# Strassen's algorithm in the input product of two middle FFNs, S5 coefficients made early, modulations on TensorE

## The chip, the cores and the metric

One Trainium2 chip, one of its cores. The metric is device time of one execution in microseconds (us). The engines of the core work side by side, each in its own order: PE (TensorE, the matrix products), DVE (VectorE), ACT (ScalarE), POOL (GpSimd), SP (SyncE, which issues most DMAs). PEld is the loading of weights into PE, a row of its own in the profile. Measured beside each other, two runs of this kernel can be told apart from about 0.2% on.

## The reference

Two layers over 512 latent and 256 context tokens, width 1024. Each layer: a SwiGLU FFN at half weight, a mixer of four head groups (S5, neighbourhood attention, GQA, RG-LRU), and a second SwiGLU FFN. Shift, scale and gate of each come from a product of the condition with `w_ada` (1024 x 9216 for each layer), the "modulations".

```python
def ada_mods(s, w, b, dt):                 # s: silu(c), one row for latents, one for context
    m = (s @ w + b)                        # 1024 -> 9 * 1024
def ffn_half(h, g, w_i, w_o, shift, scale, gate):
    y = modulate(rms_norm(h, g), shift, scale)
    a, b = jnp.split(y @ w_i, 2, axis=-1)  # w_i: 1024 x 2 * 2816
    return h + FFN_RES * gate * ((jax.nn.silu(a) * b) @ w_o)
for l in range(DEPTH):                     # latents and context alike, with their own modulations
    h = ffn_half(h, g_ffn1[l], w_ffn1_in[l], w_ffn1_out[l], m[0], m[1], m[2])
    h = h + m[5] * (mixers(modulate(rms_norm(h, g_mix[l]), m[3], m[4]) @ w_in[l]) @ w_out[l])
    h = ffn_half(h, g_ffn2[l], w_ffn2_in[l], w_ffn2_out[l], m[6], m[7], m[8])
return rms_norm(h_lat, g_final)            # the second layer's last steps: latents alone
```

The S5 group needs, for each layer, tables and weights that depend on its parameters alone (`s5_discretize` and powers of its result): the "S5 coefficients".

## The kernel before

**Products.** The residual lies transposed, eight tiles of 128 channels x 768 tokens. A float32 product is made from two parts of each operand: three products, `hi * xl`, `lo * xh`, `hi * xh` (`mm`, L389). For each weight tile of 128 x 128 and each of the three, the 768 tokens go through PE in two instructions, since one takes 512 columns at most: 258 (two of them the shifts, so that the bias comes along) and 512. The parts of the weights are made where they are needed (`wsplit`): ACT copies a tile to `wh` (L378), DVE subtracts (`wl`, L379), 1024 elements wide for eight weight tiles. `wh` and `wl` have two buffers each, so a set can be made as soon as the set before the last has been used up.

**FFN.** `ffn` goes through 22 column tiles `f` of the hidden width. For each, `ff_in` makes the gate's and the value's product (eight weight tiles each: 2 x 48 matmuls, `pi`), DVE multiplies by the norm's factor `R` (L449, L453) and combines (L455), ACT applies silu (L451) and copies the high part (L458), POOL makes the low part (L459). After each group of column tiles (`FF`: five groups of 5, 5, 4, 4 and 4) the output product of the group follows for each of eight column tiles `j` (`po`), and DVE adds it to the residual (L495). With the last group the residual of tile `j` is final: `hg_tile` makes the parts of the next stage's operand at once (ACT L304, DVE L305, squares ACT L316, their sum POOL L317), while PE goes on with `j + 1`.

**Beside it.** Closures in `hooks` are traced between column tiles. `ada_steps`: 512 columns of the modulations each (a "group" below; 32 of them: 14 in the first FFN, 9 in the second FFN of layer 0, 9 in the first of layer 1). DVE multiplies and adds 16 times (two rows, eight row blocks; L254, L256), PE sums over the partitions (L263) and transposes (L268). The first four groups' worth are made during the start on PE instead (`ada_first`, L215: two rows of weights `s2`, 512 columns moving, into four strips of 32 PSUM partitions). `S5Coef.steps`: 23 closures for each layer, in the first FFN of its own layer, `S5_AT = 7`, `S5_BY = 13`: from column tile 7 on, over 13 tiles; POOL makes the weights (L1544 to L1546), PE transposes them.

**Order.** The program is written in this order, and a scheduler with its own timeline then orders each engine's instructions; buffers are given out from pools (`wraw`: raw weights, three buffers of 8 KB a partition; `wb`: the parts). Each engine then runs its list in order: an instruction that waits holds up those behind it on its engine.

## Time and profile before

| | |
|---|---|
| device time, three runs | 2876.4, 2879.5, 2881.92 us; median 2879.5 |
| span of the profiled execution, first to last instruction | 2877.7 us |
| PE busy | 2819.1 us, 98% |
| PE's loading of weights | 2437.7 us, 85% |
| DVE busy | 1742.3 us, 61% |
| ACT busy | 906.5 us, 32% |
| POOL busy | 757.7 us, 26% |
| DMA | 312.13 MB, 31.8% of 16 engines on SP's queue |

The stages, in us from the first instruction: start to 64; first FFN of layer 0 to 655; its mixer to 945 and output projection to 1020; second FFN of layer 0 to 1607; first FFN of layer 1 to 2186; mixer to 2490; second FFN of layer 1, latents alone, to the end at 2877.7.

A busy PE is not a PE at its peak: matmuls overlap in it and their ends are modelled, so that one record of 0.4 us can follow another after 0.24. What an instruction costs PE is read from start to start. Rows of a timeline merge neighbours of the same kind (the count behind the x); a figure in square brackets is idle time ahead of the row and what ended it.

### The profile page before, as it was taken

To read this page: it belongs to the slowest core of one execution; us is meant where nothing else is said; L and a number is where in the kernel's file an instruction comes from. 1 tells how busy PE (TensorE), PEld (TensorE's weight loads), DVE (VectorE), ACT (ScalarE), POOL (GpSimd) and SP (SyncE) were. 2 spreads that over 40 slices of the span, in tenths; PEclk is the share of its full clock that TensorE was granted. 3 is DMA by queue.
4 is the path that set the end of the run, shared out by engine and by line. 5 is a ranking of instruction groups with operands and counts; after the bars stand their busy time and mean duration, and the time that the engine had idled before them with its cause. 6 is when DMAs were issued, how large, how long until landed. Compare 5 with 4: busy or idle time off the path is not lost.

```text
span 2877.7 us, 43478 instructions
## 1 busy us (share of the span) xinstructions
PE 2819.1 (98%) x17293; PEld 2437.7 (85%) x17293; DVE 1742.3 (61%) x3178; ACT 906.5 (32%) x1478; POOL 757.7 (26%) x957
## 2 busy tenths in 40 slices
PE   7999999999999999999999999999999999999998
PEld 4888888888877888888888888888888887899998
DVE  6868577676857566363634766465466876444445
ACT  4212121235546422112123321222224645322223
POOL 2822233221323311000001176332312434201001
PEclk9999999999999999999999999999999999999999
DMA  6445324353323333222311335233254343232231
GB/s 227 134 108 167 112 96 141 123 185 118 115 62 74 103 115 99 87 96 95 107 54 54 118 101 142 80 123 106 74 168 145 118 106 89 79 96 83 88 96 52
DMA packets 295901, 312.13 MB, mean 108 GB/s; under 512 B 58991, under 2 KB 243202, under 8 KB 295698
## 3 DMA queue, kind: packets, MB, share of 16 engines
q1 hardware_dynamic: 266990, 293.97, 31.8%
q0 software_dynamic: 5664, 12.59, 1.9%
q10 hardware_dynamic: 23044, 2.78, 0.7%
q8 instruction: 137, 2.24, 0.3%
q14 instruction: 66, 0.54, 0.1%
HBM read 276.09 MB, written 29.02 MB: 106 GB/s over the span
## 4 chain that ended last, share of the span: by engine, by line
PE 88%; DVE 6%; DMA 2%; ACT 2%; issue 1%; POOL 0%; SPq 0%; ACTq 0%; DVEq 0%; POOLq 0%
PE pi L389 51%; PE po L389 23%; PE po L1236 4%; DVE acc L256 2%; PE po L862 2%; PE pt L810 2%; DMA wa<-in_w_ada_dram 1%; PE ps L793 1%; PE pa L263 1%; DVE wl L379 1%; PE ps L794 1%; DMA l<-in_w_ada_dram 1%; PE pl L734 1%; DVE z L455 0%; PE pa L215 0%
## 5 line engine op out<-in xcount | busy, mean ns | idle before, releaser
L389 PE MATMUL pi<-g,wh 128*128 128x258 f32 (+2 forms) x6656 | 1408.7, 330 | 8.4 <-ACT wh L378 2.6
L389 PEld LDWEIGHTS pi<-g,wh 128*128 128x128 f32 x6656 | 1101.4, 191 | 132.2 <-issue 15.0
L389 PE MATMUL pi<-g,wl 128*128 128x258 f32 (+2 forms) x3328 | 828.1, 329 | 0.7 <-DVE wl L379 0.7
L378 ACT CAST wh<-wr 128x1024 fp32r<-128x1024 f32 (+3 forms) x380 | 338.2, 890 | 1397.4 <-PE pi L389 674.8
L389 PEld LDWEIGHTS pi<-g,wl 128*128 128x128 f32 x3328 | 607.4, 191 | 60.6 <-issue 2.5
L389 PE MATMUL po<-l,wh 128*128 128x512 f32 (+1 forms) x2464 | 566.1, 344 | 0.9 <-DVE e L495 0.8
L389 PEld LDWEIGHTS po<-l,wh 128*128 128x128 f32 x2464 | 387.9, 188 | 63.9 <-issue 3.9
L459 POOL TENSOR_TENSOR l<-z,l 128x768 fp32r<-128x768 f32 (+1 forms) x88 | 159.1, 1808 | 1061.4 <-ACT l L458 955.4
L379 DVE TENSOR_TENSOR wl<-wr,wh 128x1024 fp32r<-128x1024 f32 (+3 forms) x380 | 407.0, 1071 | 50.3 <-ACT wh L378 47.5
L256 DVE SCALAR_TENSOR_TENSOR acc<-wa,s,acc 128x512 f32<-128x512 f32 x448 | 358.6, 849 | 39.4 <-DMA wa<-in_w_ada_dram 38.6
L495 DVE SCALAR_TENSOR_TENSOR e<-po,gt,e 128x512 f32<-128x512 f32 (+1 forms) x296 | 176.2, 631 | 307.4 <-PE po L389 250.7
L389 PE MATMUL po<-l,wl 128*128 128x512 f32 (+1 forms) x1232 | 337.5, 343 | 1.0 <-DVE wl L379 1.0
L453 DVE TENSOR_TENSOR z<-pi,R 128x768 f32<-128x768 f32 (+2 forms) x91 | 78.4, 865 | 301.3 <-PE pi L389 301.3
L389 PEld LDWEIGHTS po<-l,wl 128*128 128x128 f32 x1232 | 194.5, 188 | 32.6 <-DVE wl L379 2.0
L448 DVE COPY bc<-pi 128x2 f32<-128x2 f32 x88 | 13.7, 156 | 189.4 <-PE pi L389 189.4
L458 ACT CAST l<-z 128x768 fp32r<-128x768 f32 (+1 forms) x88 | 68.8, 782 | 160.5 <-DVE z L455 160.5
L1545 POOL TENSOR_TENSOR ww<-AR,BB 128x256 f32<-128x256 f32 x32 | 25.9, 808 | 341.4 <-PE pw L1564 309.5
L455 DVE SCALAR_TENSOR_TENSOR z<-z,pi,z 128x512 f32<-128x512 f32 (+1 forms) x154 | 107.1, 730 | 5.5 <-ACT z L451 0.7
L317 POOL TENSOR_TENSOR ssq<-ssq,sq 128x768 f32<-128x768 f32 (+1 forms) x35 | 67.5, 1929 | 161.0 <-ACT sq L316 161.0
L451 ACT ACTIVATE z<-z,bc 128x512 f32<-128x512 f32 (+1 forms) x154 | 90.0, 625 | 62.7 <-DVE z L449 51.3
L449 DVE TENSOR_TENSOR z<-pi,R 128x768 f32<-128x768 f32 (+1 forms) x88 | 77.5, 880 | 3.7 <-ACT R L366 3.7
L1236 PE MATMUL po<-l,wh 128*128 128x512 f32 (+1 forms) x264 | 71.9, 356 | 0.0
(349 smaller groups left out, 2632.0 us busy)
## 6 DMA issues: line engine op xcount, KB each, us to landing
wr<-in_w_ffn_in_dram SPq DMA_DIRECT2D x88, 1024.0 KB
wa<-in_w_ada_dram SPq DMA_DIRECT2D x64, 1024.0 KB
wr<-in_w_ffn_out_dram SPq DMA_DIRECT2D x48, 512.0 KB
wr<-in_w_ffn_out_dram SPq DMA_DIRECT2D x32, 640.0 KB
wr<-in_w_in_dram SPq DMA_DIRECT2D x16, 1024.0 KB
W<-s5w SPq DMA_DIRECT2D x32, 256.0 KB
wr<-in_w_out_dram SPq DMA_DIRECT2D x8, 1024.0 KB
l<-in_w_ada_dram SPq DMA_DIRECT2D x24, 256.0 KB
```

Source lines behind the costliest of these rows:

```text
L256: nc.vector.scalar_tensor_tensor(acc[r], raw[:, k], s, acc[r], ALU.mult, ALU.add)
L378: nc.scalar.copy(hi[:, :kn], raw[:, :, o:o + P])
L379: nc.vector.tensor_sub(lo[:, :kn], raw[:, :, o:o + P], hi[:, :kn].bitcast(F32))
L389: nc.tensor.matmul(dst, lhsT=wt[:, k, :], rhs=xt[:, a:b], start=(k == 0 and i == 0), stop=(k == kn - 1 and i == 2))
L449: nc.vector.tensor_mul(ta[:, :nt], pa[:, 256:256 + nt], self.R[:, :nt])
L451: nc.scalar.activation(ta[:, a:b], ta[:, a:b], AF.Silu, bias=bc[:, i:i + 1])
L453: nc.vector.tensor_mul(tb[:, a:b], p, self.R[:, a:b])
L455: nc.vector.scalar_tensor_tensor(tb[:, a:b], tb[:, a:b], pb[:, 254 + i:255 + i], ta[:, a:b], ALU.add, ALU.mult)
L458: nc.scalar.copy(uh[:, :nt], tb[:, :nt])
L459: nc.gpsimd.tensor_sub(ul[:, :nt], tb[:, :nt], uh[:, :nt].bitcast(F32))
L495: self.nc.vector.scalar_tensor_tensor(self.h[j][:, a:b], ps[:, a:b], gate[:, j, i:i + 1], self.h[j][:, a:b], ALU.mult, ALU.add)
L1236: self.nc.tensor.matmul(dst, lhsT=wt[:, k, :], rhs=xt[:, a:b], start=(c == 0 and i == 0), stop=(c == NT - 1 and i == 2))
```

## The change

1. **Strassen** (`STRASSEN`): in the second FFN of layer 0 and the first of layer 1 the input product of a column tile is taken as a 2 x 2 by 2 x 2 product of blocks: gate and value columns, even and odd row blocks (weights: `a11`, `a12`, `a21`, `a22`, 4 x 128 elements each), first and second half of the tokens. Seven products of four row blocks, three parts and one half of the tokens (386 or 384 columns) take the place of eight: 84 matmuls a tile, where 96 were.
   - `st_weights`: four sets of weight parts a tile instead of two: `ra` (1024 wide), `s12` (1024), `ra` again after two differences in place (1024), `a22` (512). POOL makes the four sums and differences, 512 wide each.
   - `st_in`: ACT copies the first product, DVE adds the other six with seven instructions, POOL multiplies by `R` (two of 768), ACT and DVE finish as before.
   - `st_tile` in place of `hg_tile`, once for each pair of residual tiles: ACT writes the four blocks, the sums and differences of blocks go to POOL (DVE for the last pair), seven splits follow (a copy on ACT and a difference on DVE, 386 wide each).
2. **Modulations on TensorE** (`ada_steps`): for each group eight float32 matmuls, 32 columns of weights (`s2w`, the two rows and what lies behind them), 512 columns moving, into strips `32 * (k % 4)` of one bank, in place of DVE's 16 instructions; ACT copies 512 columns; four matmuls against `sel` (128 x 2, sums over the strips) replace the two transposes.
3. **S5** (`S5_AT = (5, 14)`, `S5_BY = 7`): the coefficients of both layers are made in the first FFN of layer 0, each over seven column tiles.
4. **Room**: `FF` is (4, 4, 4, 4, 3, 3), the last group three instead of four; weights are loaded 128 columns wide (rows of 512 bytes), five raw buffers of 4 KB; `wh`, `wl` two buffers and `ws` one; the `z` tiles' pool is closed in the Strassen FFNs, where their place holds operand tiles (`x`); the tokens of ordinary products go in halves (386 + 384, 384 + 384); cos and sin are loaded where they are used.

```diff
-FF = (5, 5, 4, 4, 4)
+Z_SLOTS, X_SLOTS = 5, 12
+W_BUFS = {"wh": 2, "wl": 2, "ws": 1}
+FF = (4, 4, 4, 4, 3, 3)
...
-        self.wraw = ent(tc.tile_pool(name="wraw", bufs=3))
-        self.wb = ent(tc.tile_pool(name="wb", bufs=2))
+        self.wraw = ent(tc.tile_pool(name="wraw", bufs=5))
+        self.wb = ent(tc.tile_pool(name="wb", bufs=4))
...
         def rows(k0):
-            raw = (ring() if ring else self.wraw).tile([P, 4, 512], F32, name=self.nm("wa"), tag="wraw")
-            for k in range(4):
-                for r in range(2):
-                    s = self.s2[:, k0 + k, r:r + 1]
-                    if k0 + k == 0:
-                        nc.vector.tensor_scalar_mul(acc[r], raw[:, k], s)
-                    else:
-                        nc.vector.scalar_tensor_tensor(acc[r], raw[:, k], s, acc[r], ALU.mult, ALU.add)
+            if k0 == 0:
+                st["ps"] = self.bank("pa", "pst")
+            for k in range(k0, k0 + 4):
+                if k % 2 == 0:
+                    raw = self.wraw.tile([P, 2, 512], F32, name=self.nm("wa"), tag="wraw")
...
+                o = 32 * (k % 4)
+                nc.tensor.matmul(st["ps"][o:o + 32], lhsT=self.s2w[:, 2 * k:2 * k + 32], rhs=raw[:, k % 2], start=(k < 4), stop=(k >= 4))
...
-            for i in range(4):
-                nc.tensor.matmul(ps[32 * i:32 * i + 32], lhsT=self.ones.to_broadcast([P, 32]), rhs=acc[i // 2][:, i % 2 * 256:i % 2 * 256 + 256],
-                                 start=True, stop=True)
-            nc.scalar.copy(arow, ps)
-            for b in range(2):
-                nc.tensor.transpose(pt[:, b * P:(b + 1) * P], arow[:, b * P:(b + 1) * P], self.ident)
+            nc.scalar.copy(arow, st["ps"])
+            for b in range(4):
+                nc.tensor.matmul(pt[:, 2 * b:2 * b + 2], lhsT=arow[:, b * P:(b + 1) * P], rhs=self.sel, start=True, stop=True)
...
-                ch = tuple((ps[:, a:b], (a, b)) for a, b, _ in self.segs(nt))
-                self.mm(ch, w, lambda k: u[f0 + k], fn)
+                self.mm(self.halves(ps, nt) if nt > TL else ((ps[:, :nt], (0, nt)),), w, lambda k: u[f0 + k], fn)
...
+    def st_tile(self, kk, l, mi, gs, nt, more):
...
+        X = [self.t(self.xtag.pop(0), F32R) for _ in range(7)]
...
+        def two(i, x):
+            nc.scalar.copy(hi[i], x)
+            nc.vector.tensor_sub(lo[i], x, hi[i].bitcast(F32))
+
+        E = nc.vector if kk == 3 else nc.gpsimd
+        two(0, b11)
+        two(1, b21)
+        E.tensor_sub(b11, b12, b11)
+        E.tensor_sub(b12, b22, b12)
+        two(5, b22)
+        E.tensor_sub(b22, b22, b11)
+        two(2, b22)
+        two(3, b11)
+        two(4, b12)
+        E.tensor_sub(b21, b21, b22)
+        two(6, b21)
...
+    def st_weights(self, ra, rb):
...
+        s12 = self.wtile("ws", F32)
+        s2, s1 = s12[:, :4], s12[:, 4:]
+        yield from parts(ra)
+        G.tensor_add(s1, a21, a22)
+        G.tensor_sub(s2, s1, a11)
+        yield from parts(s12)
+        G.tensor_sub(a11, a11, a21)
+        G.tensor_sub(a12, a12, s2)
+        yield from parts(ra)
+        yield from parts(a22)
+
+    def st_in(self, ra, rb, nt):
...
+            self.mm(((dst[:, :n], (0, n)),), next(ws), lambda k: self.sx[k][i], 4)
...
+        nc.scalar.copy(c21, product(0, w))
+        V.tensor_add(c11, product(1, w), c21)
+        V.tensor_add(c21, product(2, w), c21)
+        V.tensor_add(c12, product(3, m), c21[:, :m])
+        p = product(4, w)
+        V.tensor_add(c21, p, c21)
+        V.tensor_add(c22, p[:, :m], c12)
+        V.tensor_add(c12, product(5, m), c12)
+        a_, b_, R = ta[:, 2:2 + nt], tb[:, 2:2 + nt], self.R[:, :nt]
+        nc.gpsimd.tensor_mul(a_, a_, R)
...
+        V.tensor_add(c21, product(6, w), c21)
+        nc.gpsimd.tensor_mul(b_, b_, R)
...
-S5_AT = 7
-S5_BY = 13
+S5_AT = (5, 14)
+S5_BY = 7
+STRASSEN = ((0, "ffn2"), (1, "ffn1"))
...
-        for i, st in enumerate(n.s5c[l].steps()):
-            hooks[S5_FIRST[i] if i < 3 else S5_AT + (i - 3) * S5_BY // 20].append(st)
+        if l == 0:
+            for i, st in enumerate(n.s5c[0].steps()):
+                hooks[S5_FIRST[i] if i < 3 else S5_AT[0] + (i - 3) * S5_BY // 20].append(st)
+            for i, st in enumerate(n.s5c[1].steps()):
+                hooks[S5_AT[1] + i * S5_BY // 20].append(st)
```

Three places in the order that the scheduler makes of it. In these rows stand the line, the operation, output <- inputs and the output's shape.

PE in the second FFN of layer 0, where a group of modulations is finished; before: the sums over partitions (`pa`), in a row.

```order
L389 MATMUL pi_1543_9876<-g_1514_9647,wh_1541_9872 128x258
L389 MATMUL pi_1543_9876<-g_1514_9647,wh_1541_9872 128x512
L263 MATMUL pa_1553_9961<-acc_1550_9941,ones_80 32x256 x2
L263 MATMUL pa_1553_9961<-acc_1551_9943,ones_80 32x256 x2
L389 MATMUL pi_1560_9980<-g_1464_9168,wh_1558_9976 128x258
L389 MATMUL pi_1560_9980<-g_1464_9168,wh_1558_9976 128x512
```

The same place after: L424 is `mm`, L282 a pair of the new products of 512 columns; each x2 row is two row blocks.

```order
L424 MATMUL pi_1796_10775<-g_1769_10596,wl_1798_10777 128x386
L424 MATMUL pi_1796_10775<-g_1769_10596,wh_1797_10776 128x386
L282 MATMUL pa_1823_10938<-wa_1824_10939,s2w_103 32x512 x2
L282 MATMUL pa_1823_10938<-wa_1825_10943,s2w_103 32x512 x2
L424 MATMUL pi_1805_10808<-g_1700_10107,wh_1807_10810 128x386
L424 MATMUL pi_1805_10808<-g_1700_10107,wl_1808_10811 128x386
...
L282 MATMUL pa_1852_11101<-wa_1878_11252,s2w_103 32x512 x2
L291 MATMUL pt_1829_10957<-sel_107,l_1828_10955 128x2 x4
L424 MATMUL pi_1838_10990<-g_1701_10108,wh_1836_10973 128x386
```

What was one short insertion for a group is now several of 512 columns, and four products of two columns. In the whole program the 256 new products stand in 106 places (70 pairs, 18 alone, 8 of four, 6 of eight, 2 of six, 2 of three).

DVE, same stage, before: one column tile, with two sets of weights (`wl`, 1024 wide), the work on the products between them, and the modulations (`acc`).

```order
L448 COPY bc_1544_9925<-pi_1540_9823 128x2
L449 TENSOR_TENSOR z_1545_9926<-pi_1540_9823,R_84 128x768
L379 TENSOR_TENSOR wl_1559_9977<-wr_1556_9972,wh_1558_9976 128x1024
L453 TENSOR_TENSOR z_1546_9927<-pi_1543_9876,R_84 128x768
L254 TENSOR_SCALAR acc_1570_10098<-wa_1569_10096,s2_102 128x512
L254 TENSOR_SCALAR acc_1571_10100<-wa_1569_10096,s2_102 128x512
L455 SCALAR_TENSOR_TENSOR z_1546_9927<-z_1546_9927,pi_1543_9876,z_1545_9926 128x512
L455 SCALAR_TENSOR_TENSOR z_1546_9927<-z_1546_9927,pi_1543_9876,z_1545_9926 128x256
L379 TENSOR_TENSOR wl_1562_10030<-wr_1557_9974,wh_1561_10029 128x1024
```

After: one column tile with its four sets (L411), and the next one's first.

```order
L411 TENSOR_TENSOR wl_1862_11121<-wr_1855_11110,wh_1861_11120 128x1024
L627 TENSOR_TENSOR l_1833_10970<-pi_1847_11076,l_1833_10970 128x386
L411 TENSOR_TENSOR wl_1866_11155<-ws_1860_11119,wh_1865_11154 128x1024
L630 SCALAR_TENSOR_TENSOR l_1833_10970<-l_1833_10970,l_1832_10969 128x512
L630 SCALAR_TENSOR_TENSOR l_1833_10970<-l_1833_10970,l_1832_10969 128x256
L411 TENSOR_TENSOR wl_1870_11189<-wr_1855_11110,wh_1869_11188 128x1024
L616 TENSOR_TENSOR l_1857_11116<-pi_1863_11137,l_1858_11117 128x386
L617 TENSOR_TENSOR l_1858_11117<-pi_1864_11151,l_1858_11117 128x386
L618 TENSOR_TENSOR l_1857_11116<-pi_1867_11171,l_1858_11117 128x384
L411 TENSOR_TENSOR wl_1874_11225<-wr_1856_11113,wh_1873_11224 128x512
L620 TENSOR_TENSOR l_1858_11117<-pi_1868_11185,l_1858_11117 128x386
L411 TENSOR_TENSOR wl_1888_11275<-wr_1881_11264,wh_1887_11274 128x1024
```

The third set's row (`wl_1870`) stands behind L630, which waits for POOL's product with `R`.

POOL, same stage, after (before, a tile has the one instruction L459 here): sums of weights (L595 to L599), products with `R` (L624, L628), the low part (L536).

```order
L595 TENSOR_TENSOR ws_1860_11119<-wr_1856_11113 128x512
L596 TENSOR_TENSOR ws_1860_11119<-ws_1860_11119,wr_1855_11110 128x512
L536 TENSOR_TENSOR l_1822_10935<-l_1804_10807,l_1821_10934 128x768
L624 TENSOR_TENSOR l_1832_10969<-l_1832_10969,R_87 128x768
L598 TENSOR_TENSOR wr_1855_11110<-wr_1855_11110,wr_1856_11113 128x512
L599 TENSOR_TENSOR wr_1855_11110<-wr_1855_11110,ws_1860_11119 128x512
L628 TENSOR_TENSOR l_1833_10970<-l_1833_10970,R_87 128x768
```

Seven instructions a tile where one was, and the weights' sums of one tile lie between the products with `R` of another.

## Rows read from the trace of the kernel before

**Rows 1.** The page: busy time of an engine, share of the span, count.

```profile
PE 2819.1 (98%) x17293; PEld 2437.7 (85%) x17293; DVE 1742.3 (61%) x3178; ACT 906.5 (32%) x1478; POOL 757.7 (26%) x957
```

**Rows 2.** Stages: PE, PEld, DVE, ACT, POOL busy; granted clock; DMA share; GB/s.

```profile
64.00:655.00 591.00, 584.91 (x3366) 499.67 (x3366) 417.86 (x682) 141.12 (x226) 217.09 (x295) 0.99 0.43 134
...
1020.00:1607.00 587.00, 586.73 (x3361) 507.08 (x3360) 319.41 (x505) 139.79 (x199) 56.59 (x32) 1.00 0.27 88
1607.00:2186.00 579.00, 578.51 (x3353) 501.58 (x3352) 346.17 (x611) 142.19 (x226) 222.40 (x337) 1.00 0.39 120
```

**Rows 3.** Two stretches of L389 alone: PE, PEld, clock, DMA share, GB/s.

```profile
1303.00:1343.00 40.00, 40.00 (x227) 34.79 (x226) 1.00 0.32 106
2505.00:2545.00 40.00, 40.00 (x334) 40.00 (x333) 1.00 0.24 77
```

**Rows 4.** PE's timeline, start: one L215 product alone, then two (x4), and what follows.

```profile
12.91 1.02 PE L215 MATMUL pa<-l,s 128*2 128x512 f32 x2 [0.16 <-DMA l<-in_w_ada_dram]
13.87 0.66 PE L178 MATMUL px<-ident,g 128*128 128x128 f32 x4
...
44.92 1.03 PE L215 MATMUL pa<-l,s 128*2 128x512 f32 x4
45.88 0.50 PE L389 MATMUL pi<-g,wh 128*128 128x512 f32 x1
```

**Rows 5.** PE's timeline: a group's sums; its transposes; twelve passes of one column.

```profile
1058.10 0.64 PE L263 MATMUL pa<-acc,ones 128*32 128x256 f32 x8
1058.67 0.62 PE L389 MATMUL pi<-g,wh 128*128 128x258 f32 x2
...
1325.21 0.38 PE L268 MATMUL pt<-ident,z 128*128 128x128 f32 x2
1325.35 0.95 PE L389 MATMUL pi<-g,wh 128*128 128x258 f32 x4
...
1604.08 1.39 PE L357 MATMUL pr<-ones,ssq 128*128 128x1 f32 x12
1605.33 0.60 PE L389 MATMUL pi<-g,wh 128*128 128x258 f32 x2
```

**Rows 6.** PE's timeline, first FFN: waits for the modulations, and what follows.

```profile
488.09 0.62 PE L263 MATMUL pa<-acc,ones 128*32 128x256 f32 x4 [1.48 <-DVE acc L256]
488.64 0.33 PE L1559 MATMUL pw<-ident,wr 128*128 128x128 f32 x1
...
506.68 1.07 PE L263 MATMUL pa<-acc,ones 128*32 128x256 f32 x4 [2.09 <-DVE acc L256]
...
511.50 1.49 PE L389 MATMUL pi<-g,wh 128*128 128x258 f32 x4
```

**Rows 7.** Groups by form: line, engine, operation, count, busy, mean ns, idle before.

```profile
L256 DVE SCALAR_TENSOR_TENSOR acc<-wa,s,acc 128x512 f32<-128x512 f32 x448 | 358.6, 849 | 39.4 <-DMA wa<-in_w_ada_dram 38.6
L379 DVE TENSOR_TENSOR wl<-wr,wh 128x1024 fp32r<-128x1024 f32 x224 | 285.9, 1276 | 30.3 <-ACT wh L378 28.1
```

**Rows 8.** A split on DVE beside an idle POOL, then a busy one.

```profile
1330.32 1.22 DVE L379 TENSOR_TENSOR wl<-wr,wh 128x1024 fp32r<-128x1024 f32 x1
...
468.12 1.67 DVE L379 TENSOR_TENSOR wl<-wr,wh 128x1024 fp32r<-128x1024 f32 x1
```

**Rows 9.** POOL's groups by form, whole span.

```profile
L459 POOL TENSOR_TENSOR l<-z,l 128x768 fp32r<-128x768 f32 x66 | 127.2, 1927 | 736.5 <-ACT l L458 672.4 <-issue 47.1 <-DMA wa<-in_w_ada_dram 16.9
...
L459 POOL TENSOR_TENSOR l<-z,l 128x512 fp32r<-128x512 f32 x22 | 31.9, 1450 | 324.8 <-ACT l L458 283.0 <-PE po L389 21.2 <-issue 20.7
...
L749 POOL TENSOR_TENSOR l<-l,l 128x768 f32<-128x768 f32 x8 | 16.7, 2092 | 34.8 <-ACT l L747 29.8 <-DMA W<-s5w 3.7 <-PE pl L734 1.3
```

**Rows 10.** End of the second FFN of layer 0: ACT's timeline.

```profile
1595.84 1.05 ACT L378 CAST wh<-wr 128x1024 fp32r<-128x1024 f32 x1 [1.37 <-issue]
1596.80 1.12 ACT L304 ACTIVATE g<-e,gs 128x512 fp32r<-128x512 f32 x2
1597.83 0.83 ACT L316 ACTIVATE sq<-e 128x768 f32<-128x768 f32 x1
```

More of the change, by code (lines that the diff above doesn't have):

```diff
@@ new lines, in st_weights, with parts @@
+    def st_weights(self, ra, rb):
+        G = self.nc.gpsimd
+        (a11, a12), (a21, a22) = ((t[:, :4], t[:, 4:]) for t in (ra, rb))
+        def parts(w):
+            hi, lo = self.two(w)
+            for i in range(0, len(hi), 4):
+                yield hi[i:i + 4], lo[i:i + 4]
+        s12 = self.wtile("ws", F32)
[8 more added lines that the diff above has]
+        yield from parts(a22)
@@ L945, in gqa_turn @@
         n, nc = self.n, self.nc
+        cos, sin = (self.t("z", w=TL) for _ in range(2))
+        nc.sync.dma_start(cos, self.A["k_cos"])
+        nc.sync.dma_start(sin, self.A["k_sin"])
         for src in self.gts:
@@ L1622, in fin @@
                 st[key] = n.gain_scale(l, gname, m + 1)
-            n.hg_tile(j, l, m, st[key], nt)
+            if (l, key) in STRASSEN:
+                if j % 2:
+                    n.st_tile(j // 2, l, m, st[key], nt, "e" if key == "ffn2" and j < NT - 1 else "l")
+                n.sq_tile(j, nt)
+            else:
+                n.hg_tile(j, l, m, st[key], nt)
         n.ffn(l, A["w_ffn1_in"][l], A["w_ffn1_out"][l], lambda: n.gate(l, 2, 0.5), TT, fin, hooks,
               None if l else n.setup_rest)
+        if last:
+            n.room(Z_SLOTS, 0)
         n.rms_factor(TT)
@@ L1632, in body @@
         hooks = [[] for _ in range(NFF)]
[L1633 removed]
         if not last:
[L1635 removed]
+            spread(hooks, [s for q in range(ADA_2) for s in n.ada_steps(1, q)])
         end = None if last else lambda j: fin(j, 1, "ffn1", "g_ffn1", 0, TT)
[L1637 to L1639 removed]
+        n.ffn(l, A["w_ffn2_in"][l], A["w_ffn2_out"][l], lambda: n.gate(l, 8, 0.5), nt, end, hooks)
+        if last:
+            n.room(0, 0)
         if not last:
```

226 lines of the change are left out of this document (145 added, 81 removed).

## The prediction

> **What bounds the kernel now.** I read the busy times first: PE is busy for 2819.1 of 2877.7 us [rows 1], no other engine for two thirds. The stages say the same one by one: in the three FFNs of 768 tokens that the change touches PE is busy for 584.9 of 591, 586.7 of 587 and 578.5 of 579 us, and its clock is granted at 0.99 to 1.00 [rows 2]. So here time is what PE issues. DVE's 71, 54 and 60% there, and POOL's 37, 10 and 38%, cost something only where PE waits for them. What a matmul costs I take from a stretch that holds nothing but products: 227 in 40 us, 258 and 512 columns in turn, 0.176 us each, or 0.355 for two [rows 3]; those of 256 to 258 columns alone take 40 / 334 = 0.120. A matmul of 386 or 384 columns lies midway between 258 and 512 and costs 0.1775 on that line.
>
> **Strassen on PE.** A column tile's 96 matmuls cost 48 x 0.355 = 17.0 us, its 84 will cost 84 x 0.1775 = 14.9. Two stages of 22 tiles: 44 x 2.13 = **94 us less**. The output products keep their columns (384 + 384 for 512 + 256) and their price.
>
> **Modulations on PE.** Before, a group's four sums take from 1058.10 to 58.67, 0.57 us, its two transposes 0.14 [rows 5]; with about 0.1 for each break in the row of matmuls 0.9, for 32 groups 29 us. After, 512 columns move instead of 256, and eight row blocks instead of four sums. The price is in the start, where the same operation runs: one product alone takes 12.91 to 13.87, 0.96 us, and two into different strips 44.92 to 45.88, 0.96 as well [rows 4]. Strips overlap, then, and four do too: with 256 columns four sums (x8 records) take 0.57 and two (x4) 0.55 [rows 5, 6]. So what is paid is a place, whether it holds one product, two or four: 106 places x 0.96 = 102, and the six of eight and two of six products need a second round, 8 x 0.86 = 7 (0.86 is 0.96 without the break). The four products with `sel` are eight passes; twelve passes of one column take 1604.08 to 05.33, 0.104 each [rows 5], so 32 x 0.83 = 27. Together 135, less 29: **106 us more**. On PE, then, the two parts cancel: +12.
>
> **DVE.** What goes is 448 x 0.849 plus 64 first steps, some 395 us [rows 7]. By the stages' rows PE hardly waits for DVE, so this buys little directly: in the first FFN the two waits in front of the sums (1.48 and 2.09 us) and the slow stretch behind the second (four products 1.49 at 511.50, 0.95 at 1325.35) [rows 5, 6]; the two waits are 3.6, and a stretch of some 8 us at half pace behind the second costs 4: 8 to take back. With the stage's 6.1 us of idle PE in all and those 4, 10 is the most there is. The rest of DVE's time is needed by Strassen's additions.
>
> **S5 twice in the first FFN.** POOL is busy for 217 us there and for 57 in the FFN without S5 [rows 2]: 160 us a layer. Twice 160 over 7 tiles of some 29 us each, with 2 us a tile for the low parts, is 320 of 400 us, some 85% of POOL with the norm's sums, in a chain with DVE and PE's transposes. It fits, narrowly; a PE transpose at the wrong time costs a wait of the kind in [rows 6]. I take +5 (0 to 20). The 160 us that leave layer 1 make room for the POOL work that Strassen puts there, at no gain of their own, as PE was full in that stage.
>
> **Weights of the Strassen tiles.** This is the term that decides. A set of parts can be begun when its buffer is free: last matmul of the set before the last, then ACT 1.05 us [rows 10], DVE 1.22 [rows 8], and about 0.36 for hand-overs and the first matmul, which needs `wh` alone: 2.63 us. Today PE has a whole set of 48 matmuls, 8.5 us, to run meanwhile, and of its idle time little stands ahead of `pi`: 0.3 us in the whole of the second stage [rows 2]. In the new order the last set of a tile (`a22`) is one product of 12 matmuls, 2.13 us, and the next tile's first set must be made behind it. I counted, in the order of the changed program, the PE work between the release of each buffer and the first use of its successor: of 139 sets of 1024 in the two stages 47 have 2.0 to 2.6 us, 16 more up to 3.2, the others 4 and up. With 2.63 the shortfalls add up to 12 us; with splits 0.3 us later to 29, 0.5 to 42, 0.8 to 62. Later they will be: POOL's seven instructions a tile are 4 x 1.45 + 2 x 2.09 + 1.93 = 11.9 us [rows 9] in a run of tiles of 14.9, 80% busy, and a split beside a busy POOL took 1.67 against 1.22 [rows 8]. 0.8 x 0.45 is 0.36 at most, the mean of the 224 splits shows +0.05 at POOL's 26% [rows 1, 7]; I take +0.3, **+28** (12 to 62).
>
> The Trainium skill (SBUF — State Buffer, "Who interferes with whom") says that DVE and GpSimd share one port pair under an exclusive lock, the second operation being fully blocked. The row at 468.12 agrees that POOL delays a split, but by a third, not by the length of POOL's instruction; by the rule a split would wait for one of 1.45 us, half of it in the mean, and the sum of the shortfalls would be the 62.
>
> Three instructions stand in DVE's list where they can hold up a split: L630 waits for POOL's L628, itself behind another tile's sums, and the third set's `wl` is queued behind it. That chain (two POOL instructions 3.5 us, DVE's two 1.16) fits in the 4.3 us of PE's second set only when POOL is ahead; it is part of the same range.
>
> **The turn into layer 1.** `hg_tile` is a residual tile at a time today: two activations 1.12, squares 0.83, and a set's copy 1.05 [rows 10], 3 us of ACT against PE's 4.3 (24 matmuls of output product for a tile). After, for each pair of tiles, ACT has five or six block writes (2.8 us, the 1.12 of a tile and some more), seven copies of 386 (0.50 each, on the line through 0.83 for 768 and 1.05 for 1024 columns), two squares (1.7) and two copies of weights: 9 to 10 us, and POOL five differences and copies and two sums, 10 us. PE needs only 2 x 3.2 for a pair, as the last group now has three column tiles (18 matmuls). Over four pairs ACT has 38 to 42 us to do, PE 25.6 plus 6 that it can run ahead: **+10** (0 to 15), where today nothing of note is lost. The other turns with a group of three: **+3**. The same `st_tile` behind the mixer's output projection is hidden by its 75 us of products; with tiles of 9 us for a pair it may lose 2, in the range.
>
> **Loads.** The packets become shorter (512 bytes for 1 KB) at the same volume; the DMA share of the three stages is 0.27 to 0.43 [rows 2], and raw buffers hold five halves for three pairs. I cost it at nothing; if it is wrong, ACT's copy comes late in a set that has no cover, and the Strassen term grows.
>
> **Sum.** +12 - 8 + 5 + 28 + 10 + 3 = +50. The profiled execution spans 2877.7, the median of the runs is 1.8 higher: 2929.5, say **2930 us**.
>
> **Rivals.**
>
> *The cover holds.* The scheduler puts insertions of PE (modulations, output products) where the splits are late, so the 106 places lose their break (0.86, -11) and serve as cover, all 10 us of old stalls go, the sets and the turns cost 8 together: 12 - 11 - 10 + 5 + 8 = +4, 2883; with sets, turns and S5 at nothing -9, 2870. For it: a place of 0.96 is worth nearly half a missing cover, and 106 of them are placed. Against: most places lie elsewhere than at the 47 sets, as counted. It decides at a split of 2.1 us from release to first use: below that the bare product of 12 matmuls covers it. This is the rival on the other side: not slower. Chance 0.23.
>
> *POOL is the chain.* Weights' sums, products with `R` and low part at 11.9 of 14.9 us each stretch by as much as the split does (POOL too shares the delay): 1.3 x 11.9 = 15.5, more than PE's 14.9, so POOL sets the pace inside each run of tiles, and the third set is late every time. With 62 for the sets and 15 for the turn: 12 - 3 + 62 + 18 = +89, 2968. Speaking for it: two engines that slow each other [rows 8] are each over 60% busy in the run. Against: between runs PE has 26 to 34 us of output products in which POOL can catch up, three raw tiles deep. Chance 0.20.
>
> *Strassen is cheaper still or strips don't overlap* in the new place: if each of the 256 products costs 0.86 by itself, +110 more; the pairs in [rows 4] speak against it. 0.03.
>
> **How the numbers follow.** Forecast (2900 to 2957) 0.54; cover holds (2868 to 2892) 0.23; POOL's chain (2957 to 2995) 0.20; rest 0.03. The range leaves out the lower part of the first rival and the top of the second: 2872 to 2982. A measurement of this kernel can tell 0.2%, 5.8 us, from no change: below 2873.7 lies somewhat under half of the first rival, 0.10; within, most of what is left of it, 0.12; above, 0.78.
>
> **What would show it.** After, a Strassen stage should show L424's `pi` at 0.1775 a matmul between waits, L282 at 0.96 a place, and PE idle in front of the first `wl` or `wh` matmul of a tile, released by DVE or ACT, some 0.5 to 1 us each, 40-odd times. PE's busy time should be within 15 us of today's, its idle time 40 us more. If idle before `pi` is released by POOL's chain (`ws`, `wr`), the second rival is right; if PE's idle time is as today, the first. The forecast is wrong in its base if the place costs another price than 0.96, or a 386-column matmul another than 0.1775: 0.01 us on 3700 of them is 37 us.

## The result: 7.9% slower

The changed kernel takes 3106.3 us (median of four runs, 3102.5 to 3109.3), the kernel before 2878.3: the ratio is 1.079, 95% interval 1.078 to 1.081. 228 us are lost (230 in the spans of the profiled executions) where 50 were forecast, and the range ended at 2982.

The page of the changed kernel, lines that answer to [rows 1], and the granted clock in 40 slices:

```profile
PE 2923.0 (94%) x17189; PEld 2657.8 (86%) x17189; DVE 1696.3 (55%) x3036; ACT 1027.1 (33%) x1696; POOL 1126.9 (36%) x1277
...
PEclk9999999899999999999999899999999999999999
```

PE is busy for 104 us more and idle for 126 us more, where the prediction expected its busy time within 15 us and 40 us more of idle time. The stages beside [rows 2] (the columns are the same: PE, PEld, DVE, ACT, POOL busy, clock, DMA share, GB/s):

```profile
64.00:720.00 656.00, 642.36 (x3706) 599.31 (x3705) 309.03 (x771) 159.25 (x274) 350.98 (x645) 0.99 0.46 131
1075.00:1755.00 680.00, 616.96 (x3201) 559.72 (x3199) 374.22 (x496) 199.99 (x308) 274.11 (x193) 0.95 0.27 80
1755.00:2403.00 648.00, 595.57 (x3105) 538.68 (x3106) 359.04 (x478) 179.62 (x268) 241.12 (x156) 0.96 0.30 91
```

The first FFN takes longer with PE busy for all but 14 us; in the two Strassen stages PE stands still for 63 and 52 us, and the mean granted clock in them is 0.95 and 0.96, where it was 1.00. DVE's busy time rose there although the modulations left it.

For a finer account I cut the timelines at the norm's sums (L357 before, L380 after), which begin each stage, read what each matmul costs from its start to the next start, less idle time, and set the products against the price of their width (0.1775 us for 385 columns, as in the prediction). The second FFN of layer 0 went from 574.3 to 663.9: 49 us less for the products by their price, 44 more for the modulations' products, 59 more idle, 35 more for products that run slower than their price. The first FFN of layer 1, 584.8 to 661.2: 43 less, 46 more, 54 more and 29 more, and 9 less for the products of layer 1's S5, which moved away. So the saving came (92 us of the 94 forecast), and twice as much as was saved went into waits and into what follows them.

What PE waits for in the first of these stages (us in total, times, longest):

```profile
PE pt L291 <- ACT l L288: 26.2, 8, 5.0
PE pi L424 <- DVE wl L411: 9.7, 10, 1.1
PE po L424 <- DVE wl L411: 5.8, 7, 2.4
PE pi L424 <- ACT l L615: 5.6, 5, 1.3
PE pi L424 <- DVE x L566: 4.9, 1, 4.9
```

The largest is none that the prediction names: the `sel` products of a modulation group wait for ACT's copy of the sums. One of them, with the engines behind it. PE, then ACT:

```profile
1262.78 0.34 PE L424 MATMUL pi<-x,wh 128*128 128x386 f32 x1
1268.14 1.87 PE L291 MATMUL pt<-sel,l 128*128 128x2 f32 x8 [5.03 <-ACT l L288]
1269.88 0.67 PE L424 MATMUL pi<-g,wh 128*128 128x386 f32 x1
1270.34 0.53 PE L424 MATMUL pi<-g,wl 128*128 128x386 f32 x1
```

```profile
1266.77 0.83 ACT L535 CAST l<-l 128x768 fp32r<-128x768 f32 x1 [7.45 <-DVE l L630]
1267.51 0.58 ACT L288 COPY l<-pa 128x512 f32<-128x512 f32 x1
```

ACT had stood idle for 7.45 us; the copy (L288) is next in its list behind L535, which wants DVE's L630. So it is for all 18 groups of the two stages, and the last of the sums that it copies had been there for 3.4 to 45 us. In front of 17 of the 18 PE waits, for 56.3 us in all. DVE and POOL:

```profile
1256.17 2.18 DVE L411 TENSOR_TENSOR wl<-wr,wh 128x1024 fp32r<-128x1024 f32 x1 [0.52 <-ACT wh L410]
1258.27 0.55 DVE L627 TENSOR_TENSOR l<-pi,l 128x386 f32<-128x386 f32 x1
1258.74 2.12 DVE L411 TENSOR_TENSOR wl<-ws,wh 128x1024 fp32r<-128x1024 f32 x1
1263.55 3.14 DVE L630 SCALAR_TENSOR_TENSOR l<-l,l 128x512 f32<-128x512 f32 x2 [2.68 <-POOL l L628]
```

```profile
1255.72 1.55 POOL L624 TENSOR_TENSOR l<-l,R 128x768 f32<-128x768 f32 x1 [3.97 <-DVE l L622]
1258.49 1.29 POOL L598 TENSOR_TENSOR wr<-wr,wr 128x512 f32<-128x512 f32 x1 [1.22 <-DVE wl L411]
1259.75 2.26 POOL L599 TENSOR_TENSOR wr<-wr,ws 128x512 f32<-128x512 f32 x1
1261.97 1.54 POOL L628 TENSOR_TENSOR l<-l,R 128x768 f32<-128x768 f32 x1
1263.48 1.25 POOL L595 TENSOR_TENSOR ws<-wr 128x512 f32<-128x512 f32 x1
```

Read it backwards: L630 waits for POOL's L628; that stands behind L598 and L599, and L598 waits for the split at 1256.17, since it writes into what the split reads. A chain over four engines lies between this tile's products and the copy, and the copy has nothing to do with it but its place in the list. And the wait is paid again: the `sel` products at 1268.14 take 1.74 us to the next row where the same eight passes took 0.81 in the first FFN, and the matmuls behind them follow at 0.32 instead of 0.1775. The granted clock of these stretches (columns as above):

```profile
1262.80:1268.00 5.20, 0.32 (x2) 0.00 (x0) 3.14 (x2) 1.23 (x3) 3.84 (x4) 1.00 0.00 0
1268.00:1270.00 2.00, 1.85 (x9) 1.86 (x9) 0.00 (x0) 0.48 (x2) 1.23 (x1) 0.52 0.00 0
1270.00:1275.00 5.00, 5.00 (x17) 5.00 (x17) 0.94 (x3) 0.82 (x1) 0.00 (x0) 0.51 0.00 0
```

After PE has stood still for 5.03 us, the next 7 us run at the lower of its two levels (1.2 for 2.4 GHz). The same follows each of the 15 waits of 3.0 to 5.0 us in front of `sel`.

### The profile page after: what moved, and what is told of

It is laid out like the page before. It is cut to its first block, busy times and chain, and to the rows that moved or that the text cites. A ratio compares the mean times of both kernels' runs of the same rounds, so it can differ in the third digit from the quotient of the medians.

```text
span 3107.3 us, 44829 instructions
## 1 busy us (share of the span) xinstructions
PE 2923.0 (94%) x17189; PEld 2657.8 (86%) x17189; DVE 1696.3 (55%) x3036; ACT 1027.1 (33%) x1696; POOL 1126.9 (36%) x1277
## 5 line engine op out<-in xcount | busy, mean ns | idle before, releaser
L424 PE MATMUL pi<-g,wh 128*128 128x386 f32 (+3 forms) x5248 | 1220.2, 330 | 19.5 <-ACT l L615 11.1
L424 PEld LDWEIGHTS pi<-g,wh 128*128 128x128 f32 x5248 | 902.7, 193 | 81.4 <-issue 31.9
L410 ACT CAST wh<-wr 128x1024 fp32r<-128x1024 f32 (+2 forms) x456 | 371.8, 816 | 1321.0 <-PE pi L424 659.6
L424 PE MATMUL pi<-g,wl 128*128 128x386 f32 (+2 forms) x2624 | 717.5, 331 | 22.9 <-DVE wl L411 20.8
L424 PE MATMUL po<-l,wh 128*128 128x384 f32 (+2 forms) x2464 | 578.2, 346 | 6.3 <-POOL l L536 3.5
L411 DVE TENSOR_TENSOR wl<-wr,wh 128x1024 fp32r<-128x1024 f32 (+2 forms) x456 | 495.7, 1087 | 54.3 <-ACT wh L410 48.5
L424 PEld LDWEIGHTS pi<-g,wl 128*128 128x128 f32 x2624 | 471.3, 193 | 55.7 <-DVE wl L411 45.6
L424 PEld LDWEIGHTS po<-l,wh 128*128 128x128 f32 x2464 | 442.1, 189 | 41.8 <-ACT wh L410 17.6
L636 DVE SCALAR_TENSOR_TENSOR e<-po,gt,e 128x512 f32<-128x512 f32 x352 | 209.6, 631 | 322.2 <-PE po L424 292.9
L424 PE MATMUL po<-l,wl 128*128 128x384 f32 (+2 forms) x1232 | 341.3, 347 | 8.2 <-DVE wl L411 8.1
L424 PE MATMUL pi<-x,wh 128*128 128x386 f32 (+1 forms) x1056 | 336.1, 353 | 8.3 <-DVE x L566 8.3
L536 POOL TENSOR_TENSOR l<-z,l 128x768 fp32r<-128x768 f32 (+1 forms) x44 | 72.8, 1654 | 578.0 <-ACT l L535 454.3
L424 PEld LDWEIGHTS po<-l,wl 128*128 128x128 f32 x1232 | 224.5, 189 | 24.4 <-DVE wl L411 14.9
L424 PEld LDWEIGHTS pi<-x,wh 128*128 128x128 f32 x1056 | 207.6, 199 | 9.4 <-DVE x L566 9.4
L624 POOL TENSOR_TENSOR l<-l,R 128x768 f32<-128x768 f32 x44 | 70.4, 1599 | 372.0 <-DVE l L622 367.5
L424 PE MATMUL pi<-x,wl 128*128 128x386 f32 (+1 forms) x528 | 185.7, 352 | 0.0
L598 POOL TENSOR_TENSOR wr<-wr,wr 128x512 f32<-128x512 f32 x44 | 56.9, 1292 | 302.2 <-DVE wl L411 214.8
L630 DVE SCALAR_TENSOR_TENSOR l<-l,l 128x512 f32<-128x512 f32 x88 | 88.0, 1041 | 100.8 <-POOL l L628 100.8
L282 PE MATMUL pa<-wa,s2w 128*32 128x512 f32 x512 | 121.4, 610 | 10.1 <-DMA wa<-in_w_ada_dram 10.1
L424 PEld LDWEIGHTS pi<-x,wl 128*128 128x128 f32 x528 | 104.9, 199 | 0.0
```

The lines of the kernel that those rows point to most:

```text
L282: nc.tensor.matmul(st["ps"][o:o + 32], lhsT=self.s2w[:, 2 * k:2 * k + 32], rhs=raw[:, k % 2], start=(k < 4), stop=(k >= 4))
L410: nc.scalar.copy(hi, src)
L411: nc.vector.tensor_sub(lo, src, hi.bitcast(F32))
L424: nc.tensor.matmul(dst, lhsT=wt[k], rhs=xt[:, a:b], start=(k == 0 and i == 0), stop=(k == kn - 1 and i == 2))
L536: self.nc.gpsimd.tensor_sub(ul[:, :nt], tb, uh[:, :nt].bitcast(F32))
L598: G.tensor_sub(a11, a11, a21)
```

## The experiments

All stages, cut at the norm's sums, in us of the profiled run of each kernel; L0 and L1 are the layers, the mixers include the output projection, the start comes ahead and is 55 to 59. Each experiment but e11 (four runs) is one run; the runs of the kernel before that were taken beside them lie between 2878.2 and 2883.4 us (median 2880.4 beside e11), so a difference of some 5 us between two experiments shows little.

| run | FFN 1, L0 | mixer L0 | FFN 2, L0 | FFN 1, L1 | mixer L1 | FFN 2, L1 | span |
|---|---|---|---|---|---|---|---|
| before | 605.2 | 365.7 | 574.3 | 584.8 | 302.0 | 386.9 | 2877.7 |
| after | 665.4 | 365.7 | 663.9 | 661.2 | 307.0 | 388.6 | 3107.3 |
| e8 loads, groups | 606.5 | 365.9 | 576.9 | 591.3 | 313.8 | 388.4 | 2898.0 |
| e11 e8, cos and sin early | 606.1 | 369.8 | 577.0 | 591.8 | 303.7 | 387.9 | 2892.8 |
| e7 + modulations on PE | 633.8 | 368.5 | 603.5 | 615.9 | 308.6 | 388.3 | 2976.4 |
| e2 + S5 twice in one | 664.4 | 367.3 | 603.6 | 605.2 | 310.0 | 387.9 | 2993.7 |
| e1 + Strassen, `sel` later | 664.4 | 364.9 | 604.3 | 603.9 | 309.3 | 388.3 | 2992.7 |
| e3 after, modulations on DVE | 691.1 | 366.2 | 637.9 | 631.4 | 312.0 | 387.9 | 3082.7 |
| e4 after, no sums | 666.2 | 368.2 | 616.9 | 610.3 | 306.7 | 388.9 | 3014.4 |
| e5 e1, R on DVE | 666.2 | 363.2 | 601.3 | 601.2 | 314.1 | 388.4 | 2989.4 |
| e6 e1, fours | 667.4 | 365.5 | 589.7 | 586.9 | 313.2 | 388.9 | 2967.6 |
| e9 e1, three buffers | 690.9 | 366.3 | 584.6 | 585.5 | 308.3 | 387.6 | 2978.0 |
| e10 e9, R on DVE | 689.6 | 367.2 | 566.1 | 579.6 | 307.7 | 387.6 | 2954.5 |
| v3 Strassen in one stage | 606.1 | 366.2 | 626.5 | 571.2 | 308.1 | 388.1 | 2923.2 |

The rows before, e8, e7, e2, e1 and after are a ladder, a step at a time, in spans: loads and groups +20, modulations +78, S5 +17, Strassen -1, and the place of the `sel` products +115.

**e1: the `sel` products one column tile later.**

```diff
-            if k0:
-                done()
+            if k0:
+                st["arow"] = self.t("z")[:, :512]
+                nc.scalar.copy(st["arow"], st["ps"])
...
+        steps[1].after = done          # spread() hooks it behind the next column tile
```

> The changed kernel, with the four sel products of a modulation group written behind the next column tile instead of right behind ACT's copy. In the changed kernel PE stands still 17 times (56.3 us) in front of these products in the two Strassen stages, until ACT has copied the modulations (L288), and after most of these waits matmuls run at half pace for some 4 us (about 2 us lost each), the sel products too (1.73 for 0.81). Theory A (each wait costs PE by itself): all of this goes, 56 + 35 + 12, and the time is 3000 to 3015. Theory B (the chain of POOL, DVE and ACT in a Strassen tile is what is late, and PE waits for it anyhow): PE waits for a split or for a free bank of pi instead, and the time stays above 3060.

2994.5 us, 112 less: theory A, and below its range. What PE waits for in the second FFN of layer 0:

```profile
PE pi L426 <- DVE wl L413: 8.0, 9, 1.0
PE pi L426 <- ACT l L617: 7.5, 8, 1.8
...
PE pt L291 <- ACT l L285: 1.0, 1, 1.0
```

Of 17 waits in front of `sel` one of 1.0 us is left in each stage, and the clock of the stage is 0.99. Nothing else was moved in the program, and no other wait grew by more than 3 us in a stage (the one for ACT's copy of the first product from 5.5 to 8.3 in the second of them): the chain is late, but the products of the next set had buffers enough to go on.

**e2: without Strassen, all else as in the change.**

```diff
-STRASSEN = ((0, "ffn2"), (1, "ffn1"))
+STRASSEN = ()
```

> The changed kernel with ordinary input products in the two middle FFNs (96 matmuls a tile, z tiles kept); modulations on PE, S5 of both layers in the first FFN, groups and loads as in the change. Theory A (the two stages lose by waits that Strassen's splits and sums cause): without them the stages take what they took before (574 and 585 us), less the S5 products that moved away (10), plus the modulations' places, 9 x 5.1 - 8 = 38 each: 612 and 613, and the whole 3006, PE's idle time in both under 6 us; the first FFN stays at 665. Theory B (the modulations on PE bring waits wherever they are): waits for ACT's copy remain, the stages take 640 or more, the whole is 3060 or more.

2995.5 us: theory A again, with both stages 8 us below what it gave. In the second FFN of layer 0 hardly a wait is left:

```profile
PE po L424 <- DVE e L636: 1.3, 3, 0.7
PE pi L424 <- DVE wl L411: 0.7, 1, 0.7
```

The `sel` products need ACT's copy here too, but it stands in another place of ACT's list: behind a copy of weights (L410) in all 18 groups of the two stages, and done 1.4 to 4.3 us before PE comes to `sel`:

```profile
1241.61 1.05 ACT L410 CAST wh<-wr 128x1024 fp32r<-128x1024 f32 x1 [6.36 <-issue]
1242.61 0.59 ACT L288 COPY z<-pa 128x512 f32<-128x512 f32 x1
```

So neither part makes the wait alone; it takes a tile whose chain is long and a place behind it. And beside e1 it shows Strassen's balance once that wait is gone: 604.3 and 603.9 us with it, 603.6 and 605.2 without. In the two stages together the products are 90 us less by their price; 46 more of idle time, 21 of products slower than their price and 21 of more places for the modulations use that up, within what single runs can tell.

**e3: the modulations back on DVE, Strassen kept.**

```diff
...
-                nc.tensor.matmul(st["ps"][o:o + 32], lhsT=self.s2w[:, 2 * k:2 * k + 32], rhs=raw[:, k % 2], start=(k < 4), stop=(k >= 4))
...
+                        nc.vector.scalar_tensor_tensor(acc[r], raw[:, k % 2], s, acc[r], ALU.mult, ALU.add)
...
```

> The changed kernel with the modulations back on DVE (16 instructions a group, sums over partitions and transposes on PE as before), Strassen and all else as in the change. Theory A (places, sel waits and slow stretches behind them are 123 + 56 + 47 us): they go, DVE's 12 us a group cost PE little, and the time is 2885 to 2930. Theory B (DVE can't take them beside four splits a tile and a busy POOL): splits come late by more than they do now, PE's idle time in front of wl is over 100 us, and the time is 2980 or more.

3084.4 us: theory B by its time, though PE's waits for `wl` come to 62 us in the two stages and not to over 100. In the second FFN of layer 0 PE waits 34 us for `wl` and 13 each for the copies in front of the transposes and of the first product:

```profile
PE pi L428 <- DVE wl L415: 28.0, 23, 2.8
PE pt L295 <- ACT l L292: 13.0, 8, 2.7
PE pi L428 <- ACT l L619: 12.9, 6, 6.1
```

The first FFN, with S5 twice and the modulations on DVE, loses another 26: PE waits there for POOL's weights of S5 (16.7 us) and for a load of S5's (15.1). The transposes wait for ACT's copy as the `sel` products did, 13 us in each Strassen stage, and no run has them one tile later. So e3 shows what DVE makes of the modulations with that wait in it; that they had to leave DVE for Strassen's sake is likely by the waits for `wl`, and not shown.

**e4: without POOL's sums of weights.**

```diff
...
-        G.tensor_add(s1, a21, a22)
-        G.tensor_sub(s2, s1, a11)
-        yield from parts(s12)
-        G.tensor_sub(a11, a11, a21)
-        G.tensor_sub(a12, a12, s2)
+        yield from parts(rb)
...
```

> The changed kernel without POOL's four sums of weights in a Strassen tile: the sets are made from ra, rb, ra and a22 as loaded (same sizes, same number), so the products are other ones than the reference's. POOL's work in a tile falls from 7 instructions to 3. Theory A (POOL's sums slow DVE's splits and delay the third set): wl waits (30 us) nearly vanish, the mean split of 1024 falls from 1.6 us to 1.35 or less, and with the chain shorter by 5 us the waits for ACT's copy fall from 3.3 us to under 1: time 3000 to 3030. Theory B (ACT's order alone makes the copy late, whatever POOL does): sel waits stay, only wl waits go: 3060 to 3080.

This kernel leaves out the sums and so computes other products; sizes and numbers of the sets are the same. 3016.5 us, in theory A's range, but for one of its reasons only:

```profile
PE pi L424 <- DVE wl L411: 11.5, 11, 1.7
PE pt L291 <- ACT l L288: 7.8, 8, 1.3
PE po L424 <- DVE wl L411: 5.4, 7, 2.6
```

The `sel` waits fall from 3.3 to 1.0 us each, as the chain is shorter. The waits for `wl` stay (17 us for 15.5), and the mean split of 1024 is still 1.53 us. In the changed kernel 67 of the 132 splits of the two stages begin while an instruction of POOL runs, 35 of them in a sum of weights (L598, L599) and 30 in a product with `R` (L624); in e4 51 do, 34 of them in a product with `R`. Sums and products hold DVE up alike.

**e5: e1 with the products with R on DVE.**

```diff
-        nc.gpsimd.tensor_mul(a_, a_, R)
+        V.tensor_mul(a_, a_, R)
...
-        nc.gpsimd.tensor_mul(b_, b_, R)
+        V.tensor_mul(b_, b_, R)
```

> The kernel with the sel products later (2994.5 us), and the two products with R of a Strassen tile on DVE instead of POOL. Theory A (a DVE instruction that begins while one of POOL's runs waits until that one has ended: in the changed kernel the split at 1256.17 took 2.18 us beside L624 of 1255.72 to 57.27, and without POOL's sums the waits for wl stayed at 17 and 13 us, since L624 stayed): PE's waits for the first set (12 and 7 us) and for ACT's copy of the first product (7.5 and 8.3) fall by more than half, with the slow stretches behind them: 2968 to 2983. Theory B (DVE gets 42 us more in each stage and is now late by itself): 2994 or more.

2991.1 us: neither, and 3 us are within what two single runs differ by (each beside its own run of the kernel before, it is 9). The waits for ACT's copy of the first product go, from 16 us in the two stages to 2; those for `wl` grow from 19 to 24, and products slower than their price cost 8 more. In the second FFN of layer 0:

```profile
PE pi L426 <- DVE wl L413: 12.3, 20, 3.9
...
PE pi L426 <- ACT l L617: 1.0, 3, 0.7
```

64 of the 132 splits still begin inside an instruction of POOL, now a sum (32) or the low part L538 (30). Take away POOL's sums or its products, and the sets are late all the same. That left the cover itself: the work that PE has while a set is made.

**e9 and e10: three buffers of `wh` and `wl`, without and with R on DVE.**

```diff
-W_BUFS = {"wh": 2, "wl": 2, "ws": 1}
+W_BUFS = {"wh": 3, "wl": 3, "ws": 1}
-        self.wraw = ent(tc.tile_pool(name="wraw", bufs=5))
+        self.wraw = ent(tc.tile_pool(name="wraw", bufs=4))
```

> The kernel with the sel products later (2994.5 us), with three buffers each for wh and wl instead of two (and four instead of five for raw weights): a set can be begun a whole set earlier, so the 47 sets behind a single product have 6 us of matmuls for cover instead of 2.1. Theory A (the missing cover makes the waits for wl): idle PE in front of wl falls from 19 us in the two Strassen stages to under 5, and with the slow stretches the time to 2965 to 2978. Theory B (the splits are late because POOL holds DVE up, however early a set may be begun): over 15 us stay, 2985 to 2997.

> The same with three buffers, and the products with R on DVE instead of POOL (that alone: 2991.1 us, waits for ACT's copy of the first product gone, those for wl as before). Theory A (either cause alone is covered up by the other: with both taken away the two Strassen stages lose under 10 us each by waits): stages of 575 to 585 instead of 601, the whole 2945 to 2962. Theory B (DVE is now the late one, waits for wl stay): 2980 or more.

2979.8 and 2956.4 us. e9 in the second FFN of layer 0:

```profile
PE pi L426 <- ACT wh L412: 4.1, 1, 4.1
PE pi L426 <- ACT l L617: 2.5, 2, 1.4
PE pi L426 <- DVE wl L413: 2.2, 3, 1.2
```

The waits for `wl` fall from 19 us to 4 in the two stages, while the splits are hardly faster (66 of 132 begin inside an instruction of POOL, mean 1.53 us). So it was the buffers: with two, a set behind a single product of 12 matmuls isn't ready. e9's time is just above theory A's range, e10's inside it. Four raw buffers go with 26 us more in the first FFN: ACT's copies of weights wait 35 us for loads there where they waited 17 in e1, and PE 15 us for `wh`. The Strassen stages alone gain 38 in e9 and 63 in e10. 21 and 26 us of that aren't waits: in the new order the modulations' products stand more often in fours than in pairs, and their places are fewer (e6 shows the same). With 566.1 and 579.6 the stages now beat the 574.3 and 584.8 of before, the second because S5's products (9 us) have left it. Two causes covered each other, as theory A had it for e10: R on DVE bought 3 to 9 us alone and 23 with three buffers. But the stages of e10 still stand idle for 15 and 12 us, not under 10.

**e6: the modulations in fours.**

```diff
...
+                raws.append(self.wada.tile([P, 2, 512], F32, name=self.nm("wa"), tag="wada"))   # both, then the products
...
-                    raw = self.wraw.tile([P, 2, 512], F32, name=self.nm("wa"), tag="wraw")
...
+            for i in (3, 0, 1, 2):
...
```

> The kernel with the sel products later (2994.5 us), and the modulations' products in fours, one for each strip: in its order 82 places with one round each where there were 103 with 111 rounds (two buffers of their own for them, four instead of five for the weights). Theory A (a place costs 1.07 us and a further round 0.86, whether it holds one, two or four products): 21 x 0.21 + 29 x 0.86 = 29 less, 2962 to 2972. Theory B (two products share a round, four don't): no change, 2990 to 3000. If the four buffers make weights late, PE waits for DMA and it is over 3000.

2969.3 us, theory A: four strips do share a place. The products of the modulations take 21 us in each Strassen stage where e1's took 38. The changed kernel's own rows had shown it, four products (x8) in 1.00 us:

```profile
1100.07 0.34 PE L424 MATMUL pi<-g,wh 128*128 128x386 f32 x1
1100.33 1.07 PE L282 MATMUL pa<-wa,s2w 128*32 128x512 f32 x8
1101.33 0.44 PE L424 MATMUL pi<-g,wh 128*128 128x386 f32 x1
```

**e8, e7 and e11: the parts alone.** e8 takes only loads, groups and halves; e7 adds the modulations on PE; e11 is e8 with cos and sin loaded at the start again.

```diff
-S5_AT = (5, 14)
-S5_BY = 7
+S5_AT = (7, 7)                  # each layer's in its own first FFN: e7, e8, e11
+S5_BY = 13
```

> Of the whole change only the groups (4, 4, 4, 4, 3, 3), the halves of 384 to 386 tokens, the loads of 128 columns and of half a modulation block: modulations on DVE, S5 in its own layers, ordinary products. Theory A (these cost nothing, as predicted, but for 3 us at the turns): 2875 to 2886. Theory B (rows of 512 bytes make loads late, PE waits for DMA): 2895 or more.

> The kernel without Strassen and with the modulations on PE (2995.5 us), with each layer's S5 coefficients in its own first FFN as before: beside the run of loads and groups alone it shows what the modulations on PE cost by themselves, beside 2995.5 what S5 twice in one FFN costs. Theory A: S5 twice costs 6 us of PE (22 to 28 us of its products) and 3 of waits: 2984 to 2990; the modulations then cost 85 to 90. Theory B: S5 twice costs nothing, 2993 to 2999, and the modulations 95 and over.

> The run of loads and groups alone (2899.8 us beside 2883.4 of before), with cos and sin loaded at the start again. In that run the mixer of layer 1 takes 314 us for 302, and PE stands still there once for 5.4 us for a product with sin, which had waited for its load, and once for 4.2 us behind it. Theory A (the late load is most of what the loads cost): 2886 to 2893. Theory B (the groups of three and the loads in rows of 512 bytes cost it, the mixer only happens to wait at that place): 2896 to 2902.

e8: 2899.8 beside 2883.4 us, theory B by its time, but waits of PE for loads of the FFNs' weights are no part of it. The mixer of layer 1 has most:

```profile
PE pr L1093 <- DVE l L1095: 5.4, 1, 5.4
PE py L1316 <- issue: 4.2, 1, 4.2
```

L1095 multiplies with `sin`, whose load was issued 6 us earlier. e11 gets the mixer back (303.7), yet its time is 2896.5, theory B, 1.0063 of before (1.0046 to 1.0080): the rest is spread over the stages (7 us in the first FFN of layer 1, 4 in the mixer of layer 0) and wasn't taken apart further. e7: 2978.2 us, below both ranges: the modulations on PE cost 78 us without Strassen, and S5 twice in one FFN 17 (the first FFN 31 longer, layer 1's 11 shorter).

**v3: Strassen in the first FFN of layer 1 alone**, all of layer 1's modulations (on DVE) and its S5 in the FFN ahead of it, which has ordinary products.

```diff
...
+STRASSEN = ((1, "ffn1"),)
...
+            spread(hooks, [s for q in range(18) for s in n.ada_steps(1, q)])
```

> Strassen in the first FFN of layer 1 alone, with nothing beside it: all 18 groups of layer 1's modulations on DVE and layer 1's S5 coefficients stand in the second FFN of layer 0, which has ordinary products. Theory A (Strassen by itself saves 47 us a stage, and loses some 20 by splits, copies and the clock): its stage takes 550 to 560 (before: 585), the one ahead of it 592 to 600 (before: 574, plus 18 for the products of nine groups and S5), the whole 2855 to 2875. Theory B (DVE at 80% in the stage ahead makes PE wait for sums and splits, as in the first FFN with S5 twice, 58 us): 2890 or more.

2925.0 us: theory B in the stage ahead (626.5), and the Strassen stage is worse than theory A had it (550 to 560). With nothing beside it, it takes 571.2; without Strassen I estimate the 591.3 of e8 less 17 for the products of nine groups and S5, some 574. It waits:

```profile
PE pi L428 <- ACT l L619: 16.3, 10, 4.2
PE pi L428 <- DVE wl L415: 14.0, 16, 0.9
```

No run came below the kernel before. The two stages of e10 are 13 us better than before's (9 of them S5's products, which moved), but the first FFN, with S5 twice in it, modulations on PE and four raw buffers, costs 84 more than before's. e10 with the modulations in fours as in e6, or with S5 in its own layers, was not run.

## Why the prediction was wrong

**Right:** PE as the engine that sets the time, and the price of products: 49 and 43 us less in the two stages, where 47 each were expected. A place of modulations, 0.98 with 0.09 in front of it, 1.07 for 0.96; the sum, 106, was 78 without Strassen (27 us for nine groups in e7, 38 in the Strassen stages, where products stand in pairs), so about 100 in the changed kernel's own order. The waits for `wl` came to 29.5 us of idle PE for 28, for the reason given, as e9 shows; that the size fits is luck in part. The splits were 0.45 us late in the mean (1.67 for 1.22), not 0.3, and for 0.45 the prediction's own count of shortfalls (29 at 0.3, 42 at 0.5) gives some 39; and in e1, with splits as late (1.65), the waits are 19.

**Wrong, and most of the error:** the step that priced `sel` as eight passes, 0.83 a group. It put the wait in front of them, for a copy on ACT, at nothing and did not ask what stands ahead of that copy in ACT's list. I followed L630 and L628 as a chain that might hold up a split, and left it inside the range of the splits; what it held up was ACT's list, and with it PE. e1: 112 us, half of the loss. By the traces of the two stages 64 us less of PE's time are idle (54 of them in front of `sel`), 39 less go to products slower than their price and 11 less to the `sel` products themselves. The other half, by the ladder of spans, is modulations (78), S5 twice (17) and loads and groups (20), with nothing left of Strassen's saving to set against it.

**Wrong in kind:** no step had a price for what follows a wait. [rows 6] showed it (1.49 for 0.95 behind a wait of 2.09 us, at a granted clock of 0.50), and I used it only for what the first FFN might win back. In the changed kernel products slower than their price cost 36 and 31 us in the Strassen stages, 1 and 2 before.

**Wrong reading:** [rows 8], the split at 468.12. I took 1.67 for 1.22 as a share of POOL's slowing. The row of POOL beside it in the trace of before says more:

```profile
468.00 0.71 POOL L1544 TENSOR_TENSOR wt<-AI,C 128x256 f32<-128x256 f32 x1
```

POOL's instruction ended at 468.71, 0.59 after the split had begun, and the split took 0.45 more than the undisturbed 1.22: it waited for nearly all of what POOL had left. So did the one at 1256.17: POOL's L624 had 1.10 us to go, and the split took 0.96 more. Of the 132 splits of 1024 in the two Strassen stages the 67 that begin inside an instruction of POOL find 1.00 us of it left in the mean and take 2.10; the other 65 take 1.22, also those during which POOL begins something. POOL waits in the same way: L599 took 2.26 us or more the 31 times that it began with 1.12 us or more of a split left, and 1.27 to 1.28 the 9 times that DVE ran nothing at its start. The Trainium skill (SBUF — State Buffer, "Who interferes with whom") says just this, that DVE and GpSimd contend for a shared pair of ports and the one issued second is fully blocked; the prediction weighed it and judged against it, and the runs bear it out here, to within 0.12 us in the mean. (A few splits elsewhere, as the one at 2245.13 of the kernel before, beside POOL's L749, began inside a POOL instruction and took 1.21; these stay unexplained.) It would not have been enough: by the splits alone the sum was 2964.

**Wrong at zero:** loads and groups, 16 us measured beside before in e8 and 16 in e11, put down at nothing and 3. **Low:** S5 twice, 17 for 5, inside 0 to 20. The turn into layer 1, 10 predicted: PE's waits for its tiles (L566) come to 8.2 us, with 2.4 for L536 ahead of it, about the size.

**The rivals.** None reached 3107. POOL's chain was nearest, in the mechanism too, but its price was put on the third set of weights. After e1, the forecast's own Strassen balance (-94 + 28 + 10) was still 55 us too good beside e2. Of that 21 are places that the forecast had counted among the modulations; the waits for ACT's copy of the first product (16) and the products slower than their price (21 more than in e2) were in no term.

## What to carry to other kernels

Where a change lets one engine wait for a small step on another, look at what stands ahead of that step in the other's list and follow it to its end: a copy of 0.6 us cost 112 here, and writing its consumer one tile later took it away. Here PE paid for each of the long waits twice, once standing and once slow. When fewer operations stand between two uses of a buffer, count the buffers anew: the saved work was the cover.
